# Projections of a split-float32 decoder trunk: one 512-column product of the high weights for the first half of the tokens, with the low part summed apart

## The chip, the cores and the metric

The kernel runs on one core of one Trainium2 chip. The metric is the device time of one execution in microseconds. The kernel before was timed in three runs: median 3575.97 us, from 3574.45 to 3577.69 us. A further execution, the profiled one, is where every row below comes from.

## The reference

A decoder trunk of four layers (HGRN2, RWKV-7, Mamba-2, HGRN2), each followed by a SwiGLU feed-forward network (FFN), is run on 512 prompt tokens and 32 sample tokens, all in float32.

```python
D_MODEL = 1024; SEQ = 512; DEPTH = 4; DEC_BATCH = 8; DEC_SEQ = 4
D_FF = 2816

def _swiglu(h, w_gate, w_up, w_down):
    return (jax.nn.silu(h @ w_gate) * (h @ w_up)) @ w_down

def _hgrn2(h, s0, w_in, ...):
    proj = (h @ w_in).astype(F32)
    q_r, f_r, i_r, g_r = jnp.split(proj, 4, axis=-1)
    ...
    y = o.reshape(b, t, D_MODEL).astype(h.dtype) @ w_out

def _trunk(x, ...):
    for i in range(DEPTH):
        h = _rmsnorm(x, p['norm_mix'][i])
        ...
        x = x + out
        x = x + _swiglu(_rmsnorm(x, p['norm_ffn'][i]), p['ffn_w_gate'][i], p['ffn_w_up'][i],
                        p['ffn_w_down'][i])
```

Both groups of tokens go through the same weights, so the kernel puts them side by side: T = 544 columns.

## The kernel before

Activations lie with the features on the 128 partitions and the 544 tokens along the columns. A projection multiplies a weight block of 128 output features (a matrix of 8 slices of 128x128, for D_MODEL = 1024) with the activations. TensorE works here on float32r, so every float32 number is split into a high and a low part: `weights` loads a block (`wraw`), ScalarE makes the high part (`whi`, L62) and VectorE the low part (`wlo`, L64); `norm` and `split` do the same to the activations (`nh`/`nl`, `hh`/`hl`, `oa`, `yh`/`yl`). A product is three matmuls for each slice: high weights by high activations, low weights by high activations, high weights by low activations. All three are summed in one place of PSUM.

The tokens are cut in two: `HALF` is columns 0 to 255 and columns 256 to 543, so a matmul has 256 or 288 columns. The functions that the change touches are these.

- `big` takes one of two PSUM tiles of two banks (pool `psA`); the result lies in its columns 256 to 799, so that the first half fills the rest of the first bank and the second half starts the second bank.
- `proj` (L101) makes a whole product: for each slice three terms, each for both halves, 48 matmuls for 8 slices.
- `half` (L91) makes one half of a product; `pair` makes two products in the order first half of the one, first half of the other, second halves. It starts a layer, where the second half of the normalised activations is ready later. `by_half` makes the last products of a layer (the output projection, and the last group of `ffn_down`) first for the first half of all the tokens and then for the second, so that the next norm can start.
- `Part.mm` (L75) does the same for the RWKV layer, whose output projection and FFN are made for the two halves of the tokens apart; its first half has 256 columns. It lies beside the other work of that layer.

After a product the engines evacuate PSUM: in the FFN L216 and L220 (VectorE, 544 columns), in `ffn_down` L229 and L230, in the output projections L248, in HGRN2 L439 to L457, in Mamba-2 L1534 and L1745. The temporary tag `sq` has three buffers; the sums of squares in `norm` (L137 on ScalarE, L138 on GpSimd), the convolution of Mamba-2 and `Part` take turns in them. Weights have 3, 2 and 2 buffers (`wraw`, `whi`, `wlo`), so a block is split while the two before it are used. A scheduler sets the order on each engine; each engine takes its instructions in that order.

Two places hold plain 512-column float32r matmuls already: L609 (HGRN2) and L1717 (Mamba-2), which update the states of the sample sequences.

Of the kernel before, what the change touches and what calls it, by code (L numbers as in the profile page):

```python
# [23 lines left out]
WB = (3, 2, 2)  # L24


class Core:
# [51 lines left out]
    def act(self, tag, cols=T):  # L79
        return self.actp.tile([P, HW], F32R, tag=tag, name=tag)[:, 0:cols]  # L80

    def big(self):

        return self.psA.tile([P, 1024], F32, tag="big", name="big")[:, 256:256 + T]

    def half(self, ps, w, c0, xs, h, cols=P):
        hi, lo = w
        n = len(xs)
        for k, (xh, xl) in enumerate(xs):
            for a, b, first, last in ((hi, xh, k == 0, False), (lo, xh, False, False), (hi, xl, False, k == n - 1)):  # L90
                self.nc.tensor.matmul(out=ps[0:cols, HALF[h]], lhsT=a[:, k, c0:c0 + cols], rhs=b[:, HALF[h]], start=first, stop=last)  # L91

    def proj(self, w, c0, xs, cols=P):

        hi, lo = w
        ps = self.big()
        n = len(xs)
        for k, (xh, xl) in enumerate(xs):
            for a, b, first, last in ((hi, xh, k == 0, False), (lo, xh, False, False), (hi, xl, False, k == n - 1)):
                for h in range(2):  # L100
                    self.nc.tensor.matmul(out=ps[0:cols, HALF[h]], lhsT=a[:, k, c0:c0 + cols], rhs=b[:, HALF[h]], start=first, stop=last)  # L101
        return ps[0:cols]

    def pair(self, ws, xs, cols=(P, P)):

        ps = [self.big() for _ in ws]
        for h in range(2):
            for p, w, c in zip(ps, ws, cols):
                self.half(p, w, 0, xs, h, c)
        return [p[0:c] for p, c in zip(ps, cols)]  # L110
# [29 lines left out]
    def norm(self, idx):  # L140
# [3 lines left out]
        out = [(self.act(f"nh{k}"), self.act(f"nl{k}")) for k in range(KD)]  # L144
        for c in HALF:
            for k, (hi, lo) in enumerate(out):
# [56 lines left out]
    def _ffn(self, layer, fp):  # L203
# [3 lines left out]
        for g0, gn in FGRP:  # L207
            hid = []
            for m in range(g0, g0 + gn):
# [11 lines left out]
                hi = fp.tile([P, T], F32R, tag="hh", name="hh", bufs=9)  # L221
                lo = fp.tile([P, T], F32R, tag="hl", name="hl", bufs=9)
                self.split(g, hi, lo)
                hid.append((hi, lo))
# [13 lines left out]
    def by_half(self, weights, acts, add):  # L238

        for h in range(2):  # L240
            for m in range(KD):
                ps = self.big()
                self.half(ps, weights(m), 0, acts, h)
                add(m, ps, HALF[h])
# [8 lines left out]
class Part:  # L253
# [11 lines left out]
    def mm(self, w, xs):  # L265
# [4 lines left out]
        for i, (xh, xl) in enumerate(xs):  # L270
            for a, b, first, last in ((hi, xh, i == 0, False), (lo, xh, False, False), (hi, xl, False, i == n - 1)):
                self.k.mm(out=ps, lhsT=a[:, i], rhs=b, start=first, stop=last)
            if i % 2 and i < n - 1:
                yield 0
        return ps

    def halves(self, src, where, i, scale=None):
        nc = self.k.nc
        hi, lo = self.place(where, i)
# [5 lines left out]
        return hi, lo  # L285
# [51 lines left out]
class Hgrn:  # L337
# [40 lines left out]
    def _hgrn(self, layer, j, hp, first):  # L378
# [14 lines left out]
        for hd0, n in HGRP:  # L393
# [13 lines left out]
            new = [[hp.tile([P, T], F32R, tag=f"o{x}{hd0 + i}", name="oa") for x in "hl"] for i in range(n)]  # L407
            for i, ((ot, gg), (hi, lo)) in enumerate(zip(done, new)):
# [233 lines left out]
class Rwkv:  # L642
# [11 lines left out]
    def _rwkv_ffn(self, layer, rp, dp, p1, early):  # L654
        tc, nc = self.tc, self.nc
        with self.scope("rw", dict(s="01", m="2", u="e")) as pool:
# [9 lines left out]
            with tc.tile_pool(name="rw3p", bufs=1) as p3:  # L666
                with tc.tile_pool(name="rw4p", bufs=1) as p4:
                    _Samples(self, st, c, p4).run()
                places = {w: [[p3.tile([P, WIDE], F32R, name=f"{w}{n}{k}") for n in range(2)] for k in range(KD)] for w in "ax"}
# [19 lines left out]
    def _rwkv_proj(self, layer, rp, p1, px, dp):  # L689
# [36 lines left out]
        hx = [[self.act(f"n{n}{k}", HW) for n in "hl"] for k in range(KD)]  # L726
# [51 lines left out]
        def mix(n, k):  # L778
# [5 lines left out]
            self.split(t[:, 0:RV], *(x[:, o:o + RV] for x in st["act"][k]))  # L784
# [1156 lines left out]
```

## Time and profile before

| | |
|---|---|
| median of three runs | 3575.97 us |
| profiled execution | 3573.11 us |
| its span (first to last instruction) | 3571.4 us |
| mean granted TensorE clock | 0.965 |
| TensorE busy | 3332.7 us, 93% |
| VectorE busy | 2184.5 us, 61% |
| ScalarE busy | 1386.9 us, 39% |
| GpSimd busy | 857.6 us, 24% |

Busy time overlaps between engines. A matmul's recorded duration runs from its start to its modelled end and overlaps the next one's, so the time that one takes in a stream is read from start to start. The layers lie in the span in this order: HGRN2 to 388 us, its FFN to 793, RWKV-7 with its FFN to 1860, Mamba-2 to 2390, its FFN to 2788, HGRN2 to 3165, its FFN to the end.

### The profile page before, as it was taken

Reading aid. Unit: us, or ns where it says so; the run is one execution under the profiler, and the core shown is the slowest. Engines: PE = TensorE matmul, PEld = TensorE weight load, DVE = VectorE, ACT = ScalarE, POOL = GpSimd, SP = SyncE. Lnnn points to the kernel's source line nnn. Section 1 sums busy time; section 2 is a strip of 40 time slices with the busy share of each in tenths; the row PEclk is TensorE's granted clock in tenths of the full one; section 3 lists DMA queues with packets and bytes.
Section 4 is the critical chain, followed back from the end, with each engine's and each line's share of the span. In section 5 each row is a group of like instructions: output and inputs, shape, how many; then the busy total and the mean of one; then the engine's idle time right before and its main releaser. Section 6 shows DMA issues by size and latency. Waiting matters only on the chain.

```text
span 3571.4 us, 83663 instructions
## 1 busy us (share of the span) xinstructions
PE 3332.7 (93%) x35785; PEld 3147.9 (88%) x35785; DVE 2184.5 (61%) x3478; ACT 1386.9 (39%) x2364; POOL 857.6 (24%) x925
## 2 busy tenths in 40 slices
PE   8998999999888889999998888999999999899998
PEld 7887999988777778789997777999999888799998
DVE  7787543456444566776668988763344777754345
ACT  4444322245444555345343333342223444442223
POOL 5564100022223332131003533210000456410001
PEclk9999999999888899999999989999999999899999
DMA  3222322244533333554444444332222322232223
GB/s 123 80 85 92 120 88 89 89 132 148 181 118 102 107 104 113 163 192 149 160 144 115 137 134 136 118 101 89 89 87 95 108 85 84 89 121 89 89 89 108
DMA packets 190819, 405.65 MB, mean 114 GB/s; under 512 B 31712, under 2 KB 94688, under 8 KB 190448
## 3 DMA queue, kind: packets, MB, share of 16 engines
q1 hardware_dynamic: 190448, 400.30, 34.4%
q8 instruction: 282, 4.62, 0.5%
q14 instruction: 89, 0.73, 0.1%
HBM read 355.76 MB, written 43.86 MB: 112 GB/s over the span
## 4 chain that ended last, share of the span: by engine, by line
PE 46%; DVE 8%; DMA 2%; issue 2%; POOL 2%; ACT 2%; SPq 1%; POOLq 0%; DVEq 0%; ACTq 0%
PE big L101 27%; PE psp L75 10%; PE big L91 5%; DVE wlo L64 1%; DVE E L1603 1%; DVE sq L1547 1%; DMA E<-cumd 1%; DMA out_ssm_s<-E 1%; ACT whi L62 0%; DVE sq L1549 0%; DVE ql L502 0%; DVE PP L532 0%; POOL S L531 0%; PE pss L489 0%; DVE Y L1733 0%
## 5 line engine op out<-in xcount | busy, mean ns | idle before, releaser
L62 ACT ACTIVATE whi<-wraw 128x1024 fp32r<-128x1024 f32 (+2 forms) x585 | 597.5, 1023 | 1389.8 <-issue 733.8
L64 DVE TENSOR_TENSOR wlo<-wraw,whi 128x1024 fp32r<-128x1024 f32 (+2 forms) x585 | 716.9, 1226 | 196.4 <-ACT whi L62 192.2
L101 PE MATMUL big<-nl,whi 128*128 128x256 f32 (+1 forms) x3600 | 765.2, 292 | 0.8 <-issue 0.8
L101 PE MATMUL big<-nh,wlo 128*128 128x256 f32 (+1 forms) x3600 | 759.0, 291 | 2.8 <-DVE wlo L64 2.8
L101 PE MATMUL big<-nh,whi 128*128 128x256 f32 (+1 forms) x3600 | 754.1, 289 | 3.2 <-DVE raw L1534 1.6
L101 PEld LDWEIGHTS big<-nh,whi 128*128 128x128 f32 x3600 | 584.4, 190 | 12.7 <-issue 8.2
L101 PEld LDWEIGHTS big<-nl,whi 128*128 128x128 f32 x3600 | 583.9, 190 | 9.5 <-issue 8.0
L101 PEld LDWEIGHTS big<-nh,wlo 128*128 128x128 f32 x3600 | 579.4, 190 | 12.0 <-issue 6.3
L138 POOL TENSOR_TENSOR acc<-acc,sq 128x256 f32<-128x256 f32 (+1 forms) x126 | 120.5, 956 | 1640.5 <-ACT sq L137 1639.3
L75 PE MATMUL psp<-nh,whi 128*128 128x256 f32 (+1 forms) x848 | 267.0, 315 | 6.0 <-ACT nh L68 4.5
L75 PE MATMUL psp<-nh,wlo 128*128 128x256 f32 (+1 forms) x848 | 251.1, 296 | 13.0 <-DVE wlo L64 11.7
L75 PE MATMUL psp<-nl,whi 128*128 128x256 f32 (+1 forms) x848 | 250.8, 296 | 0.8 <-DVE nl L69 0.8
L220 DVE TENSOR_TENSOR fg<-fg,big 128x544 f32<-128x544 f32 x66 | 47.6, 721 | 234.9 <-PE big L101 232.4
L75 PEld LDWEIGHTS psp<-nh,wlo 128*128 128x128 f32 x848 | 169.9, 200 | 20.7 <-DVE wlo L64 14.6
L75 PEld LDWEIGHTS psp<-nh,whi 128*128 128x128 f32 x848 | 168.6, 199 | 21.0 <-ACT nh L68 5.9
L75 PEld LDWEIGHTS psp<-nl,whi 128*128 128x128 f32 x848 | 169.3, 200 | 4.5 <-issue 2.4
L216 DVE TENSOR_TENSOR fg<-big,rs 128x544 f32<-128x544 f32 x66 | 47.8, 724 | 199.3 <-PE big L101 188.5
L229 DVE TENSOR_TENSOR fd<-big,rs 128x544 f32<-128x544 f32 (+2 forms) x96 | 55.5, 580 | 178.1 <-PE big L101 159.5
L101 PE MATMUL big<-hh,wlo 128*128 128x256 f32 (+1 forms) x768 | 158.8, 288 | 0.0
L101 PE MATMUL big<-hh,whi 128*128 128x256 f32 (+1 forms) x768 | 158.0, 287 | 0.0
L101 PE MATMUL big<-hl,whi 128*128 128x256 f32 (+1 forms) x768 | 157.9, 287 | 0.0
L75 PE MATMUL psp<-x,whi 128*128 128x288 f32 x704 | 142.0, 297 | 0.0
(614 smaller groups left out, 6905.7 us busy)
## 6 DMA issues: line engine op xcount, KB each, us to landing
wraw<-in_ffn_gate SPq DMA_DIRECT2D x110, 512.0 KB, 3.2
wraw<-in_ffn_up SPq DMA_DIRECT2D x110, 512.0 KB, 3.2
wraw<-in_ffn_down SPq DMA_DIRECT2D x80, 512.0 KB, 3.5
wraw<-in_hg_in SPq DMA_DIRECT2D x64, 512.0 KB, 3.3
wraw<-in_ffn_down SPq DMA_DIRECT2D x64, 384.0 KB, 3.1
wraw<-in_rw_in SPq DMA_DIRECT2D x40, 512.0 KB, 3.8
wraw<-in_mb_in SPq DMA_DIRECT2D x40, 512.0 KB, 3.3
wraw<-in_hg_out SPq DMA_DIRECT2D x32, 512.0 KB, 3.3
```

Of the source, the lines that this page charges most:

```text
L62: nc.scalar.activation(out=hi, in_=raw, func=AF.Copy)
L64: nc.vector.tensor_tensor(out=lo, in0=raw, in1=hi.bitcast(F32), op=ALU.subtract)
L75: i = self.nc.tensor.matmul(**kw)
L91: self.nc.tensor.matmul(out=ps[0:cols, HALF[h]], lhsT=a[:, k, c0:c0 + cols], rhs=b[:, HALF[h]], start=first, stop=last)
L101: self.nc.tensor.matmul(out=ps[0:cols, HALF[h]], lhsT=a[:, k, c0:c0 + cols], rhs=b[:, HALF[h]], start=first, stop=last)
L138: (eng or nc.gpsimd).tensor_tensor(out=acc, in0=acc, in1=sq, op=ALU.add)
L216: V.tensor_tensor(out=g, in0=pg, in1=rs, op=ALU.mult)
L220: V.tensor_tensor(out=g, in0=g, in1=pu, op=ALU.mult)
L229: V.tensor_tensor(out=d[:, c], in0=ps[:, c], in1=rs[:, c], op=ALU.mult)
L1547: V.scalar_tensor_tensor(out=acc[:, s:512], in0=raw[:, 0:512 - s], scalar=cw, in1=acc[:, s:512], op0=ALU.mult, op1=ALU.add)
L1603: V.tensor_scalar(out=E[:, h], in0=E[:, h], scalar1=tok[:, 1, c, g * 8 + h:g * 8 + h + 1], scalar2=0.0, op0=ALU.subtract, op1=ALU.min)
```

## The change

The high and the low part of an activation now lie in one tile, low part first (`joint`). For the first half of the tokens the high weights meet both parts in one matmul of 512 columns, low part to columns 0 to 255 of the PSUM tile and high part to columns 256 to 511; the low weights follow with 256 columns. The low part has thus a sum of its own, and `join` adds it at the end: ScalarE copies it to an `sq` buffer, VectorE adds the copy in PSUM. The second half of the tokens (288 columns) keeps its three matmuls. `Part.mm` does likewise in its first half.

```diff
+def joint(t):
+    return t[:, 1], t[:, 0], t
...
-    def half(self, ps, w, c0, xs, h, cols=P):
-        hi, lo = w
-        n = len(xs)
-        for k, (xh, xl) in enumerate(xs):
-            for a, b, first, last in ((hi, xh, k == 0, False), (lo, xh, False, False), (hi, xl, False, k == n - 1)):
-                self.nc.tensor.matmul(out=ps[0:cols, HALF[h]], lhsT=a[:, k, c0:c0 + cols], rhs=b[:, HALF[h]], start=first, stop=last)
+        return self.psA.tile([P, 1024], F32, tag="big", name="big")
+
+    def terms(self, t, w, k, c0, x, h, cols, first, last):
+
+
+        hi, lo = (a[:, k, c0:c0 + cols] for a in w)
+        mm = self.nc.tensor.matmul
+        own = t[0:cols, 256 + HALF[h].start:256 + HALF[h].stop]
+        if h:
+            for a, b, f, l in ((hi, x[0], first, False), (lo, x[0], False, False), (hi, x[1], False, last)):
+                mm(out=own, lhsT=a, rhs=b[:, HALF[1]], start=f, stop=l)
+            return
+        both = lambda: mm(out=t[0:cols, 0:512].rearrange("p (a t) -> p a t", a=2), lhsT=hi, rhs=x[2][:, :, HALF[0]], start=first, stop=last)
+        if not last:
+            both()
+        mm(out=own, lhsT=lo, rhs=x[0][:, HALF[0]], start=False, stop=False)
+        if last:
+            both()
+
+    def join(self, t, cols):
+
+        a, b = t[0:cols, 256:512], self.tmps("sq", 3)[0:cols, 0:256]
+        self.nc.scalar.copy(out=b, in_=t[0:cols, 0:256])
+        self.nc.vector.tensor_tensor(out=a, in0=a, in1=b, op=ALU.add)
+
+    def half(self, t, w, c0, xs, h, cols=P):
+        for k, x in enumerate(xs):
+            self.terms(t, w, k, c0, x, h, cols, k == 0, k == len(xs) - 1)
+        if h == 0:
+            self.join(t, cols)
 
     def proj(self, w, c0, xs, cols=P):
 
-        hi, lo = w
-        ps = self.big()
-        n = len(xs)
-        for k, (xh, xl) in enumerate(xs):
-            for a, b, first, last in ((hi, xh, k == 0, False), (lo, xh, False, False), (hi, xl, False, k == n - 1)):
-                for h in range(2):
-                    self.nc.tensor.matmul(out=ps[0:cols, HALF[h]], lhsT=a[:, k, c0:c0 + cols], rhs=b[:, HALF[h]], start=first, stop=last)
-        return ps[0:cols]
+        t = self.big()
+        for k, x in enumerate(xs):
+            for h in range(2):
+                self.terms(t, w, k, c0, x, h, cols, k == 0, k == len(xs) - 1)
+        self.join(t, cols)
+        return t[0:cols, 256:256 + T]
...
+        L = self.L
+        for i, (xh, xl, both) in enumerate(xs):
+            if L == 256:
+
+                terms = [(ps.rearrange("p (a t) -> p a t", a=2), hi, both), (ps[:, L:], lo, xh)]
+                if i == n - 1:
+                    terms.reverse()
+            else:
+                terms = [(ps, hi, xh), (ps, lo, xh), (ps, hi, xl)]
+            for j, (o, a, b) in enumerate(terms):
+                self.k.mm(out=o, lhsT=a[:, i], rhs=b, start=i == j == 0, stop=i == n - 1 and j == len(terms) - 1)
             if i % 2 and i < n - 1:
                 yield 0
+        if L == 256:
+            t = self.tmp("sq", 3)
+            self.k.nc.scalar.copy(out=t, in_=ps[:, 0:L])
+            ps = ps[:, L:]
+            self.k.nc.vector.tensor_tensor(out=ps, in0=ps, in1=t, op=ALU.add)
         return ps
```

Over the program 3264 pairs of 256-column matmuls become one matmul of 512 columns: 1584 in the three FFNs that use `proj` and `by_half`, 640 in the two HGRN2 layers, 448 in Mamba-2 and 592 in `Part`. There are 433 joins, 76 of them in `Part`; TensorE issues 25422 matmuls where it had 28694 (the counts are those of the two programs).

On TensorE at the first product of the first layer (`pair`), the rows before are these; `nh`, `nl` are the normalised activations, the tile of the first product is the one that gets 128x288 matmuls here.

```order
L91 MATMUL big<-nh_164,whi 128x256
L91 MATMUL big<-nh_164,wlo 128x256
L91 MATMUL big<-nl_165,whi 128x256
L91 MATMUL big<-nl_151,whi 128x288
L91 MATMUL big<-nh_152,whi 128x288
L91 MATMUL big<-nh_152,wlo 128x288
```

The rows after, at the same place; `pse` is the PSUM tile of the norm, whose L195 sums the squares and whose L205 spreads the row factors.

```order
L104 MATMUL big<-n_156,wlo 128x256
L104 MATMUL big<-n_157,wlo 128x256
L101 MATMUL big<-n_157,whi 128x512
L195 MATMUL pse<-ones,acc 64x1 x4
L205 MATMUL pse<-ident,r_201 128x64 x4
L99 MATMUL big<-n_150,whi 128x288
L99 MATMUL big<-n_150,wlo 128x288
```

Before, 288-column matmuls stood directly behind the 256-column ones; now the norm's small matmuls stand between them, and the first 288-column matmul into the first tile waits for that tile's join.

On VectorE the joins of these two tiles stand here in the program after, behind the small rows of the forget-gate bounds (`lb`, `oml`).

```order
L400 TENSOR_TENSOR lb<-lb,lg 128x8
L402 TENSOR_SCALAR oml<-lb 128x16
L112 TENSOR_TENSOR big<-big,sq 128x256 x2
L197 TENSOR_SCALAR r_254<-pse 72x4
L211 RECIPROCAL r_254<-r_254 72x4
```

There was no VectorE row at that place that a matmul of the first product had to wait for.

On VectorE at the end of an FFN (the last group of `ffn_down`, first half of the tokens), the rows before are these.

```order
L229 TENSOR_TENSOR fd<-big,rs 128x256
L230 TENSOR_TENSOR x_84<-x_84,fd 128x256
L64 TENSOR_TENSOR wlo<-wraw,whi 128x768
L229 TENSOR_TENSOR fd<-big,rs 128x256
L230 TENSOR_TENSOR x_85<-x_85,fd 128x256
L64 TENSOR_TENSOR wlo<-wraw,whi 128x768
```

The rows after, at the same place.

```order
L112 TENSOR_TENSOR big<-big,sq 128x256
L252 TENSOR_TENSOR fd<-big,rs 128x256
L68 TENSOR_TENSOR wlo<-wraw,whi 128x768
L253 TENSOR_TENSOR x_84<-x_84,fd 128x256
L112 TENSOR_TENSOR big<-big,sq 128x256
L252 TENSOR_TENSOR fd<-big,rs 128x256
L68 TENSOR_TENSOR wlo<-wraw,whi 128x768
L253 TENSOR_TENSOR x_85<-x_85,fd 128x256
```

Each product has four rows where it had three, and the split of the next weights stands ahead of the addition to `x`.

## Rows read from the trace of the kernel before

**Rows 1.** The page, part 1: busy us (share of the span), instructions.

```profile
PE 3332.7 (93%) x35785; PEld 3147.9 (88%) x35785; DVE 2184.5 (61%) x3478; ACT 1386.9 (39%) x2364; POOL 857.6 (24%) x925
```

**Rows 2.** Windows: window, length, busy PE, PEld, DVE, ACT, POOL, PEclk, DMA share, GB/s.

```profile
395.00:750.00 355.00, 355.00 (x2859) 354.93 (x2858) 140.54 (x158) 89.07 (x106) 0.00 (x0) 1.00 0.27 87
750.00:793.00 43.00, 37.95 (x281) 36.25 (x280) 36.05 (x65) 22.81 (x41) 17.44 (x15) 0.96 0.62 191
1320.00:1640.00 320.00, 300.00 (x3897) 270.27 (x3896) 222.69 (x372) 144.13 (x232) 72.68 (x90) 0.98 0.48 153
1860.00:2120.00 260.00, 220.85 (x1647) 197.95 (x1645) 221.01 (x392) 90.49 (x122) 113.50 (x131) 0.91 0.43 126
2788.00:3110.00 322.00, 298.45 (x3927) 274.17 (x3927) 243.93 (x406) 133.03 (x267) 174.18 (x137) 0.97 0.25 85
```

**Rows 3.** Timeline, PE: start us, recorded us, engine line op, shapes, count.

```profile
755.82 0.28 PE L91 MATMUL big<-hh,whi 128*128 128x256 f32 x1
...
757.57 0.28 PE L91 MATMUL big<-hh,whi 128*128 128x256 f32 x1
...
21.11 0.30 PE L91 MATMUL big<-nh,whi 128*128 128x288 f32 x1
...
23.22 0.29 PE L91 MATMUL big<-nh,wlo 128*128 128x288 f32 x1
```

**Rows 4.** Timeline, PE, around the first and the last 512-column matmul in a stream.

```profile
111.88 0.39 PE L609 MATMUL pss<-vm,K 96*128 96x512 f32 x1
112.11 0.42 PE L101 MATMUL big<-nl,whi 128*128 128x256 f32 x2
...
3072.55 0.40 PE L609 MATMUL pss<-vm,K 96*128 96x512 f32 x1
3072.78 0.41 PE L101 MATMUL big<-nh,whi 128*128 128x256 f32 x2
```

**Rows 5.** Groups by line and shape: count, busy us, mean ns, idle before and releaser.

```profile
L1170 ACT COPY Y<-psm 128x256 f32<-128x256 f32 x32 | 11.5, 360 | 21.6 <-PE psm L75 21.5
L322 DVE TENSOR_TENSOR sq<-sq,psp 128x256 f32<-128x256 f32 x22 | 9.2, 418 | 6.7 <-PE psp L75 5.8
L220 DVE TENSOR_TENSOR fg<-fg,big 128x544 f32<-128x544 f32 x66 | 47.6, 721 | 234.9 <-PE big L101 232.4 <-ACT fg L217 1.6 <-PE big L91 0.9
```

**Rows 6.** Timeline, DVE and PE, start of the first layer.

```profile
22.64 0.17 DVE L366 TENSOR_SCALAR oml<-lb 128x16 f32<-128x16 f32 x1
28.00 0.72 DVE L439 TENSOR_TENSOR fr<-big,rs 128x544 f32<-128x544 f32 x1 [1.05 <-ACT rs L187]
...
16.62 0.29 PE L91 MATMUL big<-nh,whi 128*128 128x288 f32 x1
...
28.78 0.82 PE L101 MATMUL big<-nh,whi 128*128 128x256 f32 x2 [1.25 <-DVE fr L439]
29.40 0.66 PE L101 MATMUL big<-nh,wlo 128*128 128x256 f32 x2
29.85 0.66 PE L101 MATMUL big<-nl,whi 128*128 128x256 f32 x2
```

**Rows 7.** Timeline, DVE, one product of the end of the first FFN.

```profile
759.97 0.42 DVE L229 TENSOR_TENSOR fd<-big,rs 128x256 f32<-128x256 f32 x1 [0.32 <-PE big L91]
760.43 0.42 DVE L230 TENSOR_TENSOR x<-x,fd 128x256 f32<-128x256 f32 x1
760.90 0.96 DVE L64 TENSOR_TENSOR wlo<-wraw,whi 128x768 fp32r<-128x768 f32 x1
762.09 0.42 DVE L229 TENSOR_TENSOR fd<-big,rs 128x256 f32<-128x256 f32 x1 [0.23 <-PE big L91]
```

**Rows 8.** Timeline, DVE, output projection of Mamba-2, first half: four products apart.

```profile
2364.67 0.41 DVE L248 TENSOR_TENSOR o<-o,big 128x256 f32<-128x256 f32 x1
...
2371.09 0.41 DVE L248 TENSOR_TENSOR o<-o,big 128x256 f32<-128x256 f32 x1
```

**Rows 9.** The chain of waits by line, from 1860 to 2360 us, then from 2800 to 3100 us.

```profile
by line: PE big L101 36.9%; DVE E L1603 5.6%; DVE sq L1547 4.9%; DMA E<-cumd 4.5%; DMA out_ssm_s<-E 3.7%; DVE wlo L64 3.7%; issue 3.4%; DVE sq L1549 3.2%; PE big L91 2.5%; DVE Y L1733 1.7%; DMA lastd<-work 1.6%; PE psy L1659 1.6%; PE psw L1
by line: PE big L101 31.1%; issue 9.8%; DVE ql L502 4.9%; DVE PP L532 4.9%; POOL S L531 4.3%; DVE wlo L64 3.1%; PE pss L489 2.9%; POOL kl L510 2.1%; POOL Q L452 2.1%; POOL s L603 1.6%; PE big L91 1.5%; DVE md L542 1.5%; PE pss L617 1.3%; AC
```

More of the change, by code (lines that the diff above doesn't have):

```diff
@@ L104, in pair @@
     def pair(self, ws, xs, cols=(P, P)):
-        ps = [self.big() for _ in ws]
+        ts = [self.big() for _ in ws]
         for h in range(2):
-            for p, w, c in zip(ps, ws, cols):
-                self.half(p, w, 0, xs, h, c)
-        return [p[0:c] for p, c in zip(ps, cols)]
+            for t, w, c in zip(ts, ws, cols):
+                self.half(t, w, 0, xs, h, c)
+        return [t[0:c, 256:256 + T] for t, c in zip(ts, cols)]
     def setup(self):
@@ L241, in by_half @@
             for m in range(KD):
-                ps = self.big()
-                self.half(ps, weights(m), 0, acts, h)
-                add(m, ps, HALF[h])
+                t = self.big()
+                self.half(t, weights(m), 0, acts, h)
+                add(m, t[:, 256:256 + T], HALF[h])
     def out_proj(self, weights, acts):
@@ L278, in halves @@
         nc = self.k.nc
-        hi, lo = self.place(where, i)
+        hi, lo, both = self.place(where, i)
         if scale is None:
@@ L406, in _hgrn @@
             V.reciprocal(out=r, in_=r)
[L407 to L408 removed]
+            new = [joint(hp.tile([P, 2, T], F32R, tag=f"o{hd0 + i}", name="oa")) for i in range(n)]
+            for i, ((ot, gg), (hi, lo, _)) in enumerate(zip(done, new)):
                 o = ot[:, 0:4]
@@ L668, in _rwkv_ffn @@
                     _Samples(self, st, c, p4).run()
-                places = {w: [[p3.tile([P, WIDE], F32R, name=f"{w}{n}{k}") for n in range(2)] for k in range(KD)] for w in "ax"}
+                places = {w: [joint(p3.tile([P, 2, WIDE], F32R, name=f"{w}{k}")) for k in range(KD)] for w in "ax"}
                 part = Part(self, HALF[1], lambda where, k: places[where][k], "p", lambda: self.bank("p", [P, WIDE]),
@@ L725, in _rwkv_proj @@
         hs = [p1.tile([P, HW], F32, name=f"h{k}") for k in range(KD)]
-        hx = [[self.act(f"n{n}{k}", HW) for n in "hl"] for k in range(KD)]
+        hx = [self.act(k, HW)[0:2] for k in range(KD)]
         dx = []
@@ L800, in spill @@
             return t
-        st["act"] = [[self.act(f"n{n}{k}") for n in "hl"] for k in range(KD)]
+        st["act"] = [self.act(k) for k in range(KD)]
         xk = []
@@ L881, in _rwkv_main @@
         at = dict(a=0, x=WIDE)
-        place = lambda where, k: [t[:, at[where]:at[where] + 256] for t in st["act"][k]]
-        part = Part(self, HALF[0], place, "p", lambda: self.bank("p", [P, 256]), lambda: self.tmps("sq", 3)[:, 0:256])
+        place = lambda where, k: joint(st["act"][k][2][:, :, at[where]:at[where] + 256])
+        part = Part(self, HALF[0], place, "p", lambda: self.bank("p", [P, 512]), lambda: self.tmps("sq", 3)[:, 0:256])
         proj = _Steps(self._rv(st))
```

30 lines of the change are left out of this document (12 added, 18 removed).

## The prediction

> **What bounds the kernel now.** I read the page first: TensorE is busy for 93% of the span, VectorE for 61% [rows 1]. That average hides stages with different limits, so the windows by stage come next. Inside an FFN TensorE is busy for 355.00 of 355 us at a granted clock of 1.00, the level of 2.4 GHz, and VectorE for 141: nothing but the stream of matmuls counts there. At the end of an FFN it is 38 of 43 us with VectorE at 36, in the RWKV layer's `Part` 300 of 320 with VectorE at 223, in Mamba-2 221 of 260 with VectorE at 221 too, in HGRN2 298 of 322 with VectorE at 244 [rows 2]. There added VectorE work can reach the end. The timeline of TensorE gives the price of a matmul in a stream, from start to start; the groups by shape give the joins' prices and what VectorE waits for; the chain of waits says how often VectorE is what is waited for.
>
> **What merging two matmuls gives.** Sixteen starts of 256 columns follow one another from 755.82 to 757.57: 15 steps, 0.1167 us each. Seventeen of 288 columns go from 21.11 to 23.22: 16 steps, 0.1319 each [rows 3]. Two of 256 columns are thus 0.233. Plain 512-column matmuls in float32r exist already: in 31 places of L609 and L1717 another `big` matmul follows one at once, after 0.230 to 0.241, mean 0.2355; the first and the last of these stand in [rows 4] (111.88 to 112.11, 3072.55 to 3072.78). So two matmuls and one of twice the width take the same time: I take 0. Two bounds. If the step from 256 to 288 columns (0.0152 for 32) goes on, 512 take 0.1167 + 8 x 0.0152 = 0.238, which loses 0.005 for each of 3264 pairs, 16 us. If only a part that each matmul pays once is saved and every further column costs one cycle of 2.4 GHz, 512 take 0.1167 + 256/2400 = 0.223, and 3264 x 0.010 = 33 us are saved. The direct rows lie between and are the nearest, though their weights have 96 rows and not 128.
>
> The Trainium skill (TensorE: Matmul & The Clock Gate, section "Wait — 56ns, not 53.3ns?") states that a matmul at the full clock takes its columns at 2.4 GHz and some 2.5 ns besides. By that the merge would save about 3264 x 2.5 ns = 8 us, an estimate from that page, and my sum would end 8 us lower, at 3588. The trace does not agree with it for this data type: 0.1167 where the rule gives 0.109, 0.2355 where it gives 0.216.
>
> **What a join costs.** ScalarE's copy of 128x256 from PSUM takes 0.360 (L1170), VectorE's add from PSUM 0.418 (L322) [rows 5]. With the gaps of 0.04 between VectorE's rows [rows 7] I count 0.46 us of VectorE for each join. The 433 joins are 199 us of VectorE and 156 us of ScalarE; what matters is where they lie.
>
> *Inside the FFNs*: 0. A product takes 24 x (0.1167 + 0.1319) = 5.97 us. VectorE waits 234.9 us before its 66 L220, 3.6 us each, nearly all for TensorE [rows 5]. The evacuation starts about 0.36 + 0.42 + 0.2 = 1 us later, and with its own 0.72 the PSUM tile is free 1.7 us after the product; the other tile keeps TensorE busy for 5.97. Queued behind ScalarE's copy is the high part of a block that is used two products later. Were this cover gone, the 1 us would stand in full before each product.
>
> *Starts of layers (`pair`)*. In the first layer the 288-column matmuls ran from 16.62 on, and `fr` of the first head was evacuated at 28.00 [rows 6]. Now the first of them waits for its tile's join, which VectorE has behind `oml` (22.64, 0.17): it ends at about 22.64 + 0.17 + 0.42 = 23.2. Then 48 x 0.1319 = 6.3 us of matmuls and the norm's small ones (about 0.6) lead to 30.2, which is 2.2 later. TensorE has idled before that, and the rows show what this does: after the idle time before 28.78 the pairs of 256 and 288 columns stand 0.45 apart (29.40, 29.85) where they take 0.25, and this repeats at another place. I take 3; bounds 2 and 5. In the other five starts the second tile's first half (2.8 us of TensorE) lies between a join's release and its use: 0, at most 1 each.
>
> *Ends of FFNs*. A product of the first half has 18 matmuls, 18 x 0.1167 = 2.10, and VectorE's rows repeat after 2.12 with 0.23 of waiting for TensorE [rows 7]. A join brings VectorE to 2.12 - 0.23 + 0.46 = 2.35, so VectorE sets the pace: 0.23 for each of 8 products, of which the buffered weights hide about two. 6 x 0.23 x 3 FFNs = 4; bounds 0 (the queue of weights covers it) and 9 (each copy's 0.36 besides, in one product of two).
>
> *End of Mamba-2*. Four products take 2371.09 - 2364.67 = 6.42, 1.605 each [rows 8], though TensorE needs 12 x 0.1167 = 1.40: VectorE sets the pace already. 0.46 more for 7 products is 3; bounds 2 and 5. In HGRN2's output projection a product has 24 matmuls, 2.80, and VectorE has room: 0.
>
> *HGRN2 heads*. 64 joins lie in the two layers' heads, 64 x 0.46 = 29 us. VectorE's lines that the chain of 2800 to 3100 shows (`ql`, `PP`, `wlo`, `md`) hold 4.9 + 4.9 + 3.1 + 1.5 = 14.4% of it [rows 9]. If added work lengthens the chain in that share, 29 x 0.144 = 4. Bounds: 0, if it all falls into VectorE's idle time, and 29.
>
> *Mamba-2's groups*. 65 joins, 30 us. The chain of 1860 to 2360 has VectorE (`E`, both `sq`, `wlo`, `Y`) with 5.6 + 4.9 + 3.2 + 3.7 + 1.7 = 19.1% [rows 9]: 30 x 0.191 = 6. Bounds 0 and 30. The copies take `sq` buffers that the convolution uses too.
>
> *`Part`*. 76 joins, 35 us. A product takes 24 x 0.1167 = 2.8 us, its evacuation with the join about 1.4, and there are two buffers: 0. VectorE is busy for 70% here [rows 2], so up to a third of it, 10, could show.
>
> **Sum**: 0 + 3 + 4 + 3 + 4 + 6 + 0 = +20 us. On the profiled execution's 3573.1 that is 3593. The median of the runs lies 2.9 above the profiled execution, so for a median 3596.
>
> **The rivals.**
> *The wide matmul is cheaper than the rows say.* If 512 columns take 0.223, the FFNs, where only the stream counts, give 1584 x 0.010 = 16 us; of the other 17 I count 10, since their stages also wait for others. With half to all of the 20 us of joins, the time is 3576 - 26 + 10 to 20 = 3560 to 3570, middle 3565. It decides for faster when a 512-column matmul falls below 0.2334 - 20/3264 = 0.227. For it: a matmul may pay something once. Against it: 31 places, none below 0.230. The Trainium skill's rule of 2.5 ns (same page and section) is a weaker form of it; its 3588 lies inside the forecast's range.
> *The joins are hidden nearly everywhere.* VectorE is busy for 61% [rows 1], and only the waits of the first layer's start and of Mamba-2's end, 3 + 3, remain: 3576 to 3583, middle 3580. For it: idle VectorE time in each stage. Against it: at the FFNs' ends and in Mamba-2 VectorE has almost none.
> *The joins stand in the chain.* A copy waits for an `sq` buffer or for its turn on ScalarE, the add for the copy, and whole stages slip: half of the upper bounds of HGRN2, Mamba-2 and `Part` (15 + 15 + 5) and 5 + 9 + 5 of starts and ends, 54 in all: 3630, from 3612 up.
>
> **How the numbers follow.** My forecast (3584 to 3612, middle 3596) has 0.53, the cheaper wide matmul 0.17, the hidden joins 0.18, the joins in the chain 0.12. About 0.2%, 7 us, is what a measurement of this kernel can tell from no change: below 3569 is faster, above 3583 slower. The cheaper matmul is faster in most of its cases (0.15), and 0.02 goes to a gain that I don't see; the hidden joins are the same (0.18), with 0.02 of the cheaper matmul's; slower is the rest, 0.63. For 8 in 10 the range takes the forecast, the hidden joins, the upper half of the cheaper matmul and a little of the chain: 3562 to 3616.
>
> **What the profile after would show.** In a timeline inside an FFN, a group of one 512-, one 256- and three 288-column matmuls lasts 0.235 + 0.117 + 0.396 = 0.748, as the six before do (3 x 0.2486 = 0.746), and the FFN's stretch keeps its length within 2 us; 0.736 or less would make the first step wrong. `fr` of the first head is evacuated 2 to 4 us later than 28.00. At the end of an FFN VectorE's rows repeat after about 2.35 without waits for TensorE. VectorE's busy time rises by about 181 us, ScalarE's by 156. The layers HGRN2 and Mamba-2 are longer by a few us each; if they keep their lengths, the shares of the chain were a bad measure, and if they grow by 10 or more, waits for `sq` or for the copies should stand before the joins.

## The result and the profile after

The changed kernel takes 3719.09 us in the median of four runs (3714.38 to 3721.23), the kernel before 3576.83 us beside it; the ratio is 1.0401, with an interval from 1.0386 to 1.0416. The profiled execution has a span of 3716.3 us, 144.9 more than before, at a mean granted clock of 0.958.

The page, part 1, of the changed kernel answers to [rows 1].

```profile
PE 3387.7 (91%) x32513; PEld 3023.4 (81%) x32513; DVE 2330.8 (63%) x3911; ACT 1528.2 (41%) x2798; POOL 850.6 (23%) x925
```

VectorE has 146 us more and ScalarE 141, less than the 181 and 156 that were counted for the joins: the amount of added work is not what was misjudged. TensorE is busy for 55 us more, though it issues fewer matmuls. The rest of the 145 us is time in which TensorE waits. Windows of the changed kernel: the heads of the first HGRN2 layer, the first FFN from its first gate to its last, Mamba-2, the heads of the last HGRN2 layer; columns as in [rows 2].

```profile
33.40:386.10 352.70, 304.38 (x3576) 263.39 (x3576) 247.59 (x427) 142.10 (x294) 169.14 (x136) 0.93 0.21 73
445.30:793.00 347.70, 347.70 (x2299) 326.44 (x2298) 155.55 (x209) 104.67 (x157) 0.00 (x0) 1.00 0.26 87
1932.10:2443.60 511.50, 450.40 (x3016) 387.20 (x3017) 420.18 (x753) 196.76 (x308) 171.37 (x186) 0.95 0.39 118
2894.30:3246.60 352.30, 304.58 (x3586) 263.09 (x3584) 249.17 (x427) 141.16 (x294) 169.45 (x136) 0.93 0.21 73
```

In HGRN2 VectorE is busy for 70% of the window, where it was 76% in [rows 2]: this is no engine that became the bound. The FFN is still all TensorE at the full clock, and 4.6 us longer than the 343.0 that the same lines span before. The same cut of the heads in the kernel before:

```profile
28.00:339.80 311.80, 287.39 (x3832) 262.88 (x3832) 237.13 (x394) 129.66 (x261) 172.93 (x136) 0.97 0.23 81
2798.30:3110.40 312.10, 288.55 (x3841) 264.13 (x3839) 239.45 (x397) 129.76 (x263) 173.38 (x136) 0.97 0.24 82
```

The table gives all stages, cut at the first or last start of an evacuation (`fr`, the output projection's addition, the FFN's first product, `fd`, `Part`'s first gate and last `fd`); "own" is the version e7 of the experiments, "no join" is e6.

| stage, us | before | changed | own | no join |
|---|---|---|---|---|
| start to the first `fr` | 28.0 | 33.4 | 33.0 | 29.2 |
| HGRN2 heads, first layer | 311.8 | 352.6 | 321.2 | 319.4 |
| HGRN2 heads, last layer | 312.1 | 352.3 | 324.0 | 314.9 |
| three FFNs, first to last gate | 1029.2 | 1042.8 | 1026.6 | 1028.1 |
| three FFN ends | 170.0 | 176.0 | 175.3 | 169.1 |
| RWKV-7 up to `Part`'s first gate | 524.2 | 540.3 | 537.0 | 525.6 |
| `Part` | 541.8 | 545.8 | 543.7 | 534.7 |
| Mamba-2 without its output projection | 500.4 | 511.5 | 509.6 | 495.9 |
| three output projections | 153.8 | 161.4 | 158.5 | 155.3 |

The heads of the two HGRN2 layers hold 81 of the 145 us. By the windows TensorE idles 48 us more in them and is busy for 33 us longer, at a mean granted clock of 0.93 where it was 0.97; how much of the 33 is the clock was not separated. TensorE's own waits name the place of the idle time. The chief line of the waits, engine PE, whole span:

```profile
PE big L101 <- DVE fr L475: 37.0, 15, 2.6
```

In fourteen of the sixteen heads, all but the first of each layer, TensorE stands for 2.6 us until `fr` of the head is evacuated (the fifteenth wait of the line, 0.9 us, is at the start of the first layer, where [rows 6] have one of 1.25). The timeline of one such place on ScalarE:

```profile
158.24 0.37 ACT L664 COPY R<-pss 128x256 f32<-128x256 f32 x1 [1.89 <-PE pss L663]
158.63 0.60 ACT L635 ACTIVATE sq<-pse 128x512 f32<-128x512 f32 x1
159.12 0.58 ACT L636 COPY ot<-pse 128x512 f32<-128x512 f32 x1
159.59 0.67 ACT L111 COPY sq<-big 128x256 f32<-128x256 f32 x2
```

On VectorE:

```profile
160.01 0.43 DVE L112 TENSOR_TENSOR big<-big,sq 128x256 f32<-128x256 f32 x1
...
161.54 0.43 DVE L112 TENSOR_TENSOR big<-big,sq 128x256 f32<-128x256 f32 x1
161.88 0.26 DVE L637 TENSOR_REDUCE ss<-sq 32x1 f32<-32x128 f32 x1
162.07 0.70 DVE L475 TENSOR_TENSOR fr<-big,rs 128x544 f32<-128x544 f32 x1
```

On TensorE, the last matmul of the second of the two products, and the next product:

```profile
154.87 0.29 PE L99 MATMUL big<-n,whi 128*128 128x288 f32 x1
...
162.92 0.47 PE L101 MATMUL big<-n,whi 128*128 128x512 f32 x1 [2.58 <-DVE fr L475]
```

Both products of the next head lie ready in PSUM at 155. Their joins' copies are issued at 159.59, both at once, right behind L635 and L636, in which ScalarE squares the output of the head before into an `sq` buffer and copies it. The joins take their buffers from that same tag, and in the program the head before asks for its buffer ahead of them. ScalarE's rows have this order at all fourteen places. Until then both PSUM tiles are full, so TensorE has no place for another product, and the next head can't begin beside the end of the last one.

### The profile page after: what moved, and what is told of

Same layout as the page of the kernel before. It is cut to its first block, busy times and chain, and to the rows that moved or that the text cites. A ratio compares the mean times of both kernels' runs of the same rounds, so it can differ in the third digit from the quotient of the medians.

```text
span 3716.3 us, 77971 instructions
## 1 busy us (share of the span) xinstructions
PE 3387.7 (91%) x32513; PEld 3023.4 (81%) x32513; DVE 2330.8 (63%) x3911; ACT 1528.2 (41%) x2798; POOL 850.6 (23%) x925
## 4 chain that ended last, share of the span: by engine, by line
PE 40%; DVE 10%; DMA 3%; ACT 3%; issue 2%; POOL 2%; SPq 0%; POOLq 0%; DVEq 0%; ACTq 0%
PE big L99 15%; PE big L101 9%; PE psp L79 8%; PE big L104 5%; DVE wlo L68 1%; DVE E L1639 1%; DMA out_ssm_s<-E 1%; DMA E<-cumd 1%; DVE sq L1583 1%; ACT whi L66 1%; DVE big L112 0%; DVE PP L568 0%; POOL acc L163 0%; DVE ql L538 0%; DMA E<-in_st_ssm 0%
## 5 line engine op out<-in xcount | busy, mean ns | idle before, releaser
L99 PE MATMUL big<-n,whi 128*128 128x288 f32 x3792 | 1086.9, 303 | 2.1 <-DVE big L112 2.1
L101 PE MATMUL big<-n,whi 128*128 128x512 f32 x1896 | 773.4, 410 | 57.0 <-DVE fr L475 37.0
L99 PEld LDWEIGHTS big<-n,whi 128*128 128x128 f32 x3792 | 723.1, 192 | 82.1 <-issue 3.6
L99 PE MATMUL big<-n,wlo 128*128 128x288 f32 x1896 | 576.4, 304 | 0.0
L104 PE MATMUL big<-n,wlo 128*128 128x256 f32 x1896 | 540.6, 286 | 0.7 <-DVE wlo L68 0.7
L101 PEld LDWEIGHTS big<-n,whi 128*128 128x128 f32 x1896 | 366.3, 193 | 72.5 <-issue 47.6
L99 PEld LDWEIGHTS big<-n,wlo 128*128 128x128 f32 x1896 | 368.3, 194 | 14.0 <-issue 2.2
L104 PEld LDWEIGHTS big<-n,wlo 128*128 128x128 f32 x1896 | 365.5, 193 | 5.4 <-issue 2.3
L79 PE MATMUL psp<-n,whi 128*128 128x512 f32 (+1 forms) x1104 | 354.2, 376 | 14.8 <-ACT n L72 5.8
L99 PE MATMUL big<-hid,whi 128*128 128x288 f32 x1056 | 276.3, 296 | 0.2
L79 PE MATMUL psp<-n,wlo 128*128 128x256 f32 (+1 forms) x848 | 237.9, 295 | 5.7 <-DVE wlo L68 5.7
L101 PE MATMUL big<-hid,whi 128*128 128x512 f32 x528 | 204.6, 399 | 4.6 <-ACT sq L111 4.3
```

What stands on the lines that cost most here:

```text
L79: i = self.nc.tensor.matmul(**kw)
L99: mm(out=own, lhsT=a, rhs=b[:, HALF[1]], start=f, stop=l)
L101: both = lambda: mm(out=t[0:cols, 0:512].rearrange("p (a t) -> p a t", a=2), lhsT=hi, rhs=x[2][:, :, HALF[0]], start=first, stop=last)
L104: mm(out=own, lhsT=lo, rhs=x[0][:, HALF[0]], start=False, stop=False)
```

## The experiments

Ratios are to the kernel before in runs beside them. "us" is the ratio's distance from 1 times 3575.

| run | what it is | ratio (interval) | us |
|---|---|---|---|
| changed kernel | | 1.0401 (1.0386 to 1.0416) | +143 |
| e1 | joins with buffers of their own | 1.0211 (1.0196 to 1.0227) | +75 |
| e2 | wide matmuls, no joins | 1.0055 (1.0040 to 1.0070) | +20 |
| e3 | joins, no wide matmuls | 1.0507 (1.0489 to 1.0524) | +181 |
| e4 | before, halves apart within a slice | 0.9987 (0.9977 to 0.9996) | -5 |
| e5 | changed, padded row | 1.0383 (1.0366 to 1.0400) | +137 |
| e6 | e2, padded row | 1.0005 (0.9994 to 1.0016) | +2 |
| e7 | e1, padded row | 1.0173 (1.0158 to 1.0189) | +62 |
| e8 | before, `nh` shifted by 4 bytes | 1.0079 (1.0062 to 1.0096) | +28 |
| e9 | e6, two `sq` buffers | 0.9994 (0.9985 to 1.0003) | -2 |
| e10 | e6, VectorE's part alone | 1.0056 (1.0034 to 1.0077) | +20 |
| e11 | e3, padded row | 1.0467 (1.0443 to 1.0490) | +167 |
| e12 | e9, ScalarE's copies alone | 0.9973 (0.9961 to 0.9986) | -10 |
| e13 | e7, the add without the copy's data | 1.0176 (1.0160 to 1.0191) | +63 |
| e14 | e7, copies on VectorE | 1.0251 (1.0232 to 1.0269) | +90 |
| e15 | two sums, no wide matmuls, no joins | 1.0038 (1.0024 to 1.0052) | +14 |
| e16 | e7, copy and add without any tie | 1.0128 (1.0108 to 1.0149) | +46 |
| e18 | e10, two `sq` buffers | 1.0063 (1.0046 to 1.0080) | +23 |

**e1, buffers of their own.** There is no room for three more buffers, so `sq` gives one up.

```diff
-        a, b = t[0:cols, 256:512], self.tmps("sq", 3)[0:cols, 0:256]
+        a, b = t[0:cols, 256:512], self.tmp.tile([P, 256], F32, tag="jn", name="jn", bufs=2)[0:cols]
...
-        sq = self.tmps("sq", 3)
+        sq = self.tmps("sq", 2)
```

> The joins' copies get buffers of their own (two, tag jn); sq keeps two instead of three, since there is no room for more. Theory A (the shared tag: a join of the next HGRN2 head has to wait its turn in sq behind the squares of the head before, so that two heads no longer overlap): the 82 to 86 us that the two HGRN2 layers' heads lost come back for the most part, heads every 36 to 37 us again instead of 40.5, and the time falls from 3719 to 3640 to 3660. Theory B (the joins' own work on ScalarE and VectorE stands in the chain, whatever buffer they use): 3700 to 3720, heads every 40 us.

3652.07 us: 68 of the 143 us come back. The heads' windows shrink from 352.6 and 352.3 to 319.0 and 324.7, so 61 of the 68 lie there. Theory A holds, theory B does not: the joins' work was all still there. In the kernel before the heads overlapped; VectorE evacuated `fr` of the fourth head 25 us before it reduced the squares of the third.

```profile
128.87 0.72 DVE L439 TENSOR_TENSOR fr<-big,rs 128x544 f32<-128x544 f32 x1
...
154.23 0.67 DVE L601 TENSOR_REDUCE ss<-sq 128x4 f32<-128x512 f32 x1
```

How they overlap again is seen in VectorE's timeline of e7, which has the same buffers.

```profile
129.48 0.41 DVE L112 TENSOR_TENSOR big<-big,jn 128x256 f32<-128x256 f32 x1
129.93 0.72 DVE L475 TENSOR_TENSOR fr<-big,rs 128x544 f32<-128x544 f32 x1
...
159.69 0.68 DVE L637 TENSOR_REDUCE ss<-sq 128x4 f32<-128x512 f32 x1
```

The fourth head's join and `fr` are done at 130, thirty microseconds before the squares of the third head are reduced (L637, 159.69). In the changed kernel the fourth head's `fr` (162.07) stood behind that reduction, as in each of the fourteen heads. That the order of the requests ties the heads, and not that three buffers are too few, is read from these timelines: e1 and e7 overlap with one `sq` buffer less, but with two more for the copies, and no version gave the shared tag more buffers.

**e2, no joins; e3, no wide matmul; e4, the order alone.**

```diff
     def join(self, t, cols):
-        a, b = t[0:cols, 256:512], self.tmps("sq", 3)[0:cols, 0:256]
-        self.nc.scalar.copy(out=b, in_=t[0:cols, 0:256])
-        self.nc.vector.tensor_tensor(out=a, in0=a, in1=b, op=ALU.add)
+        return
```

> The 512-column matmuls without the joins: the sum of the low part is left out of the result. Theory A and B alike put nearly the whole loss on the joins: 3585 to 3600, of which some 16 us are a stream that runs at 0.757 us for a slice in the FFNs where it was 0.746. If the wide matmuls themselves lose time elsewhere (their operands, their order, PSUM), 3620 or more.

3595.38 us: without the joins 20 us stay, so those 20 belong to the matmuls or to the place of their operands.

```diff
-        both = lambda: mm(out=t[0:cols, 0:512].rearrange("p (a t) -> p a t", a=2), lhsT=hi, rhs=x[2][:, :, HALF[0]], start=first, stop=last)
...
+        mm(out=t[0:cols, 0:256], lhsT=hi, rhs=x[1][:, HALF[0]], start=first, stop=False)
+        mm(out=own, lhsT=hi, rhs=x[0][:, HALF[0]], start=False, stop=False)
+        mm(out=own, lhsT=lo, rhs=x[0][:, HALF[0]], start=False, stop=last)
```

> The joins without the wide matmul: the high weights meet the low and the high part in two matmuls of 256 columns, the low part in its own sum, and the join stays as in the changed kernel. If the loss is the joins', 3700 to 3725. If the wide matmul is what costs, 3600 to 3640.

3757.23 us, above what either theory said: the joins without the wide matmul cost more than with it.

```diff
-            for a, b, first, last in (...):
-                for h in range(2):
+            for h in range(2):
+                for a, b, first, last in (...):
```

> The kernel before with another order inside proj: for each slice three matmuls of 256 columns and then three of 288, instead of the halves in turn. If it is three 288-column matmuls in a row that made the FFN's slice 0.757 instead of 0.746, 3588 to 3595; if it is the 512-column matmul, 3574 to 3579.

3569.7 us: three 288-column matmuls in a row cost nothing. This is the only version here with the whole computation that is not slower than the kernel before; its gain is 0.13% (0.04 to 0.23).

**e5 to e8, where the high part starts.** A row of the joint tile was 553 long, so the high part began at byte 4 x 553 = 2212. e5, e6 and e7 are the changed kernel, e2 and e1 with this line:

```diff
-        return joint(self.actp.tile([P, 2, HW], F32R, tag=f"n{k}", name=f"n{k}")[:, :, 0:cols])
+        return joint(self.actp.tile([P, 2, 560], F32R, tag=f"n{k}", name=f"n{k}")[:, :, 0:cols])
```

e8 is the kernel before with its `nh` tiles shifted:

```diff
-        return self.actp.tile([P, HW], F32R, tag=tag, name=tag)[:, 0:cols]
+        o = int(tag[1] == "h")
+        return self.actp.tile([P, HW + 1], F32R, tag=tag, name=tag)[:, o:o + cols]
```

> The changed kernel with one size changed: a row of the joint activation tile is 560 float32 long instead of 553, so that the high part starts at byte 2240, a multiple of 64, and not at 2212. Theory C (the high part's start off such a boundary slows each matmul that streams it; in the FFNs a slice of `n` takes 0.757 us where the bytes before took 0.746, and 288-column matmuls on `n` are recorded at 303 ns against 296 on `hid`, whose parts start at 2176): an FFN's stretch from the first gate to the last goes from 348.8 back to 343 to 344 us, the whole kernel 12 to 22 us down, 3697 to 3707. Theory D (two sums in one PSUM bank, or 512 columns, are what slows the stream): no change, 3714 to 3724.

> The wide matmuls without the joins (the sum of the low part is left out) and with the padded row. By theory C nothing of the change is left that costs, and the 512-column matmul gives nothing: 3572 to 3582, as before. By theory D 3590 to 3600, as without the padding. If the wide matmul does save something once it is well placed: below 3570.

> Joins with buffers of their own and the padded row: by theory C 3630 to 3642 (the 3652 of the joins with buffers of their own, less 10 to 22), by theory D 3648 to 3656. What stays above the kernel before is the joins' own work and the sq buffers that went from three to two.

> The kernel before, with nothing changed but the place of the high activations `nh`: they start one float32 (4 bytes) into a tile one float32 longer. By theory C two thirds of the matmuls on `n` slow down as in the changed kernel: 3588 to 3600, the FFN's stretch 346 to 349 us instead of 343.3. By theory D nothing: 3572 to 3579.

Theory C holds in all four, though e8's 3602 us lie 2 above its range: the shift cost more than expected, 7 us in each FFN's gates (350.3 against 343.0). In the first FFN's gates (530 to 740 us) 288-column matmuls on the shifted `nh` follow after 0.136 us where it was 0.131, those on `nl`, which was not shifted, after 0.132 as before; 256-column ones on `nl` went from 0.118 to 0.121. In e5 the gates gain what theory C said (347.6 to 343.0 us in each FFN), but the whole only 6 of the 12 to 22 us that were expected. A slice in the FFN of the changed kernel, TensorE's timeline:

```profile
499.88 0.40 PE L101 MATMUL big<-n,whi 128*128 128x512 f32 x1
500.12 0.28 PE L104 MATMUL big<-n,wlo 128*128 128x256 f32 x1
500.23 0.30 PE L99 MATMUL big<-n,whi 128*128 128x288 f32 x1
500.37 0.30 PE L99 MATMUL big<-n,wlo 128*128 128x288 f32 x1
500.51 0.30 PE L99 MATMUL big<-n,whi 128*128 128x288 f32 x1
500.64 0.40 PE L101 MATMUL big<-n,whi 128*128 128x512 f32 x1
```

And of e5:

```profile
500.15 0.40 PE L101 MATMUL big<-n,whi 128*128 128x512 f32 x1
500.38 0.28 PE L104 MATMUL big<-n,wlo 128*128 128x256 f32 x1
500.50 0.29 PE L99 MATMUL big<-n,whi 128*128 128x288 f32 x1
500.63 0.29 PE L99 MATMUL big<-n,wlo 128*128 128x288 f32 x1
500.76 0.29 PE L99 MATMUL big<-n,whi 128*128 128x288 f32 x1
500.90 0.39 PE L101 MATMUL big<-n,whi 128*128 128x512 f32 x1
```

0.76 against 0.75 for a slice, and the three 288-column matmuls go from 0.41 to 0.40. With the row padded the wide matmuls are worth nothing, neither way (e6), and e8 makes the kernel before 28 us slower with a shift of 4 bytes and no other change.

**e9 to e12, what is left of the joins (e7 above e6: 60 us).** e9 is e6 with two `sq` buffers, by the last two lines of e1's diff, wherever `sq` is asked for. e10 is e6 with, in place of a join (in `Part` likewise),

```diff
+        a, b = t[0:cols, 256:512], self.ones[0:cols, 0:1].to_broadcast([cols, 256])
+        self.nc.vector.tensor_tensor(out=a, in0=a, in1=b, op=ALU.mult)
```

e11 is e3 with the line of e5, and e12 is e7 without the add:

```diff
         self.nc.scalar.copy(out=b, in_=t[0:cols, 0:256])
-        self.nc.vector.tensor_tensor(out=a, in0=a, in1=b, op=ALU.add)
```

> Wide matmuls, padded row, no joins (the sum of the low part is left out), and the sq tag with two buffers instead of three. The joins with buffers of their own had to pay for them with one of the sq buffers; if that is what keeps them 57 us above the version without joins, this one is at 3600 to 3630. If it is the joins' work or the wait for it, the two buffers cost little: 3572 to 3585.

> Wide matmuls, padded row, three sq buffers; in place of each join VectorE alone multiplies the 256 columns of PSUM by a column of ones: the same place, operation kind and size as the join's add, but no copy on ScalarE and no buffer (the sum of the low part is left out). Theory V (VectorE's added 181 us are what costs): 3610 to 3632. Theory H (the hand-over from TensorE to ScalarE to VectorE is what costs, each a turn in a queue held in order): 3580 to 3600.

> Joins in the sq tag and the padded row, with two 256-column matmuls of the high weights in place of the wide one. If the wide matmul is worth nothing, as the version without joins says, 3698 to 3715 like the padded changed kernel. If it hides something that only counts beside the joins (the unpadded pair stood 38 us apart), 3730 to 3750.

> Wide matmuls, padded row, ScalarE's copies into buffers of their own and two sq buffers, but without VectorE's add (the sum of the low part is left out of the result). If ScalarE's copies hold up its queue: 3590 to 3615. If ScalarE has room (41% busy) and only the add or the wait for both counts: within 8 us of the version with two sq buffers and no joins.

The missing `sq` buffer costs nothing (e9). VectorE's part alone costs 20 us, the copies alone cost nothing (e12; why it is 8 us faster than e9 is not known), and both together 60. e10 fell in theory H's range, but that did not make the hand-over the cause yet. e11 stays 30 us above e5: beside the joins the wide matmul is worth something against two narrow ones.

**e13 to e16 and e18, hand-over or work.** e13 is e7 with an add that reads no copy:

```diff
-        self.nc.vector.tensor_tensor(out=a, in0=a, in1=b, op=ALU.add)
+        self.nc.vector.tensor_tensor(out=a, in0=a, in1=self.ones[0:cols, 0:1].to_broadcast([cols, 256]), op=ALU.mult)
```

e16 is e13 with a copy that reads no product:

```diff
-        self.nc.scalar.copy(out=b, in_=t[0:cols, 0:256])
+        self.nc.scalar.copy(out=b, in_=self.ones[0:cols, 0:1].to_broadcast([cols, 256]))
```

e14 is e7 with the copy on the other engine:

```diff
-        self.nc.scalar.copy(out=b, in_=t[0:cols, 0:256])
+        self.nc.vector.tensor_copy(out=b, in_=t[0:cols, 0:256])
```

e15 is e11 with e2's diff, and e18 is e10 with the last two lines of e1's.

> The joins with buffers of their own and the padded row (3632), with one operand changed: VectorE multiplies by a column of ones and no longer reads ScalarE's copy, so both instructions are still issued for each join, but neither waits for the other (the sum of the low part is left out of the result). Theory H (what costs 57 us there is the hand-over, VectorE's queue standing still until ScalarE's queue has come to the copy): 3580 to 3605. Theory V (the two engines' work together): 3620 to 3635.

> The joins with buffers of their own and the padded row, with the copy on VectorE instead of ScalarE: VectorE does some 150 us more, and the hand-over between the engines is gone. Theory H: below 3632, 3600 to 3625, though VectorE has more to do. Theory V: 3640 to 3680.

> No wide matmul, the low part in a sum of its own, padded row and no joins at all (its sum is left out of the result). If two sums in one PSUM bank slow the 256-column matmuls, the FFN's stretch is 350 us as with the joins (350.6) and the whole 3590 to 3605. If the 38 us that the wide matmul is worth beside the joins come from the joins, the stretch is 342 to 344 and the whole 3570 to 3580.

> Both instructions of a join, with nothing between them: ScalarE copies a column of ones to the jn buffer instead of the low sum, VectorE multiplies the 256 columns of PSUM by a column of ones, so that each engine has the work of the padded version with buffers of its own (3632), VectorE waits for TensorE alone and nobody waits for the copy (the sum of the low part is left out). In the version where only the operand was changed VectorE still waited for the copy, because both touched the same PSUM tile. Theory H (of the 57 us, 21 are the adds and the rest is VectorE's wait for the copy): 3585 to 3605. Theory V (the work of both engines): 3620 to 3640.

> The version with VectorE's multiply alone in place of a join (3596, three sq buffers), with two sq buffers, as the versions with buffers of their own have them. If the third sq buffer is what the pair of instructions lacks beside VectorE's added work, 3610 to 3622, like the version with both instructions apart (3619). If ScalarE's copies make that difference, 3592 to 3602.

e13 told nothing of the hand-over: in its program VectorE still waits for the copy, since both touch one PSUM tile. e16 takes the tie away. The waits, engine DVE, of e7 and then of e16 show that it did:

```profile
DVE big L112 <- ACT jn L111: 599.5, 201, 4.3
```

```profile
DVE big L112 <- PE big L99: 594.8, 200, 4.1
```

Of e7's 62 us above the kernel before, 46 stay in e16 (3618.92 us, a little under theory V's range and well over theory H's). The hand-over, with the copy's own wait for TensorE, is thus some 16, and theory H is wrong as the main cause. The rest comes with the work of both engines: 20 to 23 for the adds alone (e10, e18), and as much again when ScalarE has its copies too, though these alone cost nothing. e14, with 90, is the slowest of the versions with buffers of their own: 150 us more of VectorE cost more than the hand-over. In which queue the two loads meet was not settled. The scheduler also orders every version anew, and no run tells work from order here: in e16 the heads of the first layer take 330.2 us and those of the last 317.7, in e7 321.2 and 324.0.

e15 answers half of the other question. Without any join, two 256-column matmuls and a sum of its own for the low part cost 14 us, most of it in the FFNs' gates (346.5 against 343.0 in each), as e11's are 347.5; both the time and the gates lie between the two expectations. So the wide matmul makes up for a loss that the split into two sums brings, and it gains nothing over the single sum of the kernel before. That the loss comes of two sums in one PSUM bank is not shown. TensorE's timeline of e15, and then of e4, which has one sum and the halves apart too:

```profile
599.93 0.28 PE L101 MATMUL big<-n,whi 128*128 128x256 f32 x1
...
600.28 0.30 PE L99 MATMUL big<-n,whi 128*128 128x288 f32 x1
...
600.68 0.28 PE L101 MATMUL big<-n,whi 128*128 128x256 f32 x1
```

```profile
599.92 0.29 PE L101 MATMUL big<-nh,whi 128*128 128x288 f32 x1
...
600.31 0.28 PE L101 MATMUL big<-nh,whi 128*128 128x256 f32 x1
...
600.67 0.29 PE L101 MATMUL big<-nh,whi 128*128 128x288 f32 x1
```

On `n` the three 256-column matmuls take 0.35 and 0.36; it is the three 288-column ones, which go to one sum in the other bank, that take 0.40 where it was 0.39 (0.401 and 0.390 in the mean of some 210 slices). On `hid` it is the 256-column ones (0.360 against 0.354). e15 also has another order of weights, high, high, low, and no run tells the two apart. The other 16 of the 30 us between e11 and e5 lie in `Part` and the FFNs' ends (563.5 against 552.0, and 57.3 against 51.7 in the first FFN), and why stays open.

## Why the prediction was wrong

The forecast was 3596 with a range up to 3616; the kernel takes 3719. Slower was the right sign, the size was off by a factor of seven.

**The step that failed** is "HGRN2 heads": added VectorE work was to lengthen the chain in VectorE's share of it, 4 us, at most 29. Measured are 40.8 and 40.2. The bound was that of VectorE's work, and the cost was an order: the copies share the tag `sq` with the squares at a head's end, so a head's first two joins stand behind the end of the head before. e1 shows it: the same joins in other buffers give 68 us back, 61 of them in the heads. The sum named the shared buffers only for Mamba-2's convolution. A shared buffer was treated as a wait of a buffer's length, where it tied two pieces of the program that had overlapped. The third rival, "the joins stand in the chain", came nearest, with 3630 and with `sq` in it; it was still too small, since it took half of the bounds of work. The sign that the prediction set for this case, ten or more us in a layer and `sq` or the copies ahead of the joins, is what the profile shows. The share of the chain was too small a measure for the joins' work as well: with buffers of their own the heads still stand 20 us above the kernel before, where 4 were counted, though inside the bound of 29.

**The wide matmul, 0**: right for the whole. It follows at 0.23 to 0.24 in its new places too (499.88 to 500.12; 500.15 to 500.38), and e6 is at 1.0005. The rival in which it saved 26 us falls. By the 2.5 ns of the Trainium skill (TensorE: Matmul & The Clock Gate, section "Wait — 56ns, not 53.3ns?") 3264 x 2.5 ns = 8 us, an estimate from that page, would be saved. The whole kernel does not show them, since e6's interval ends at 0.9994. A few us in the FFNs are not excluded: their gates take 1028.1 us in e6 and 1025.4 in e9 against 1029.2, where e4's order alone gives 1027.6. (By the counts of 28694 and 25422 matmuls the merged pairs are 3272 and not 3264; nothing here turns on that.)

**A slice in the FFN**: predicted at 0.748, measured at 0.76, and by the whole stage 4.6 us for each FFN's gates. The price of the matmuls was right for rows that start where they did; that the joint tile moves the start of the high part to byte 2212 was not seen as a part of the change. It cost 18 to 20 us without the joins (e2 against e6: 20 and 2), 13 with buffers of their own (e1 against e7), and only 6 in e5: there the gates are 14 us shorter, but RWKV-7 with `Part` is 7 and Mamba-2 4.5 us longer in the profiled execution, and why is not known.

**Inside the FFNs, joins 0**: right. The gates of e7, with all joins and the padded row, last 1026.6 us, of the kernel before 1029.2.

**The start of the first layer**: predicted 3, bounds 2 and 5; measured 5.4. The step was right, the size a little over its bound. Timeline of the changed kernel, VectorE and TensorE:

```profile
23.46 0.92 DVE L112 TENSOR_TENSOR big<-big,sq 128x256 f32<-128x256 f32 x2
...
33.43 0.72 DVE L475 TENSOR_TENSOR fr<-big,rs 128x544 f32<-128x544 f32 x1 [1.30 <-ACT rs L212]
```

```profile
23.93 0.61 PE L99 MATMUL big<-n,whi 128*128 128x288 f32 x1 [2.12 <-DVE big L112]
```

The first 288-column matmul waits for the join, as said, until 23.9 (said: 23.2). What was left out is behind it: `fr` starts on the row factors `rs`, as it did in [rows 6], and not on the product alone.

**Ends of FFNs**: predicted 4 through a pace of 2.35 us that VectorE sets; measured 6 for all three, but not by that. VectorE's timeline of the changed kernel, against [rows 7]:

```profile
808.70 0.43 DVE L112 TENSOR_TENSOR big<-big,sq 128x256 f32<-128x256 f32 x1 [0.29 <-ACT sq L111]
809.16 0.42 DVE L252 TENSOR_TENSOR fd<-big,rs 128x256 f32<-128x256 f32 x1
809.51 0.95 DVE L68 TENSOR_TENSOR wlo<-wraw,whi 128x768 fp32r<-128x768 f32 x1
810.37 0.42 DVE L253 TENSOR_TENSOR x<-x,fd 128x256 f32<-128x256 f32 x1
810.86 0.43 DVE L112 TENSOR_TENSOR big<-big,sq 128x256 f32<-128x256 f32 x1
```

The rows repeat after 2.16, not 2.35: they overlap in their starts (809.16 to 809.51 for a row of 0.42), so the sum of durations overstated VectorE's need. The pace gives 8 x 0.04 x 3 = 1 of the 6; that 4 came near is luck, and where the other 5 lie was not followed up.

**End of Mamba-2**, predicted 3: its output projection is longer by 4.3 (37.0 to 41.3). **Mamba-2's groups**, predicted 6: 11.1, inside the bounds. **`Part`**, predicted 0, at most 10: 4. **RWKV-7 before `Part`'s FFN** had no term at all, and lost 16. Its output projection has joins in `Part`. Without joins it is 530.6 (e2), with the padded row besides 525.6 against 524.2; but beside the joins the padding gives nothing there (540.9 in e5 against 540.3).

So the 143 us, taken apart in this order, are three things: the shared buffers 68 (changed kernel against e1), the joins' work and hand-over 55 (e1 against e2), and the start of the high part 20 (e2 against the kernel before, 18 of them gone in e6). In another order the parts differ, as e5's 6 us for the third show. The prediction had 20 for the second and nothing for the first and the third.

## What to carry to other kernels

A temporary taken from a tag that others use can be an edge in the program's order, not only a wait for memory: look up who has the tag before and behind, and whether work that overlaps now would stand in one line. When two operands are put into one tile, check at which byte the second now starts. And before matmuls are merged to make them wider, read from start to start whether a wide one in the same data type takes less than two narrow ones.

## What the runs showed of the hardware

Float32r matmuls followed one another more slowly when their moving operand started elsewhere: the kernel before lost 0.79% (0.62 to 0.96) when `nh` started 4 bytes further on (e8), and padding a row from 2212 to 2240 bytes took the gates of an FFN from 347.6 to 343.0 us at a granted clock of 1.00. The Trainium skill (SBUF — State Buffer, section "Door 1: The DMA port swizzle") tells of lines of 16 bytes and a penalty for each crossing. Both slow starts, byte 4 and byte 2212 of a tile, lie 4 bytes off such a line if the tile itself starts on one, which no trace shows; with that the runs agree with it in sign. Which boundary counts was not tried.

The costs of added work on two engines did not add up: the copies alone -10 us (e12), the adds alone +20 to +23 (e10, e18), both without any tie +46 (e16).
